# Turning two chunks of both heads with one full transpose in a hybrid encoder trunk

## The chip, the cores and the metric

The kernel runs on one core of a Trainium2 chip. A core has five engines that run their own instruction queues in order and meet at semaphores: TensorE (PE, matrix products into PSUM, with its weight loads shown apart as PEld), VectorE (DVE), ScalarE (ACT), GpSimd (POOL) and SyncE (SP, which here only issues DMAs). The metric is the time of one execution on the device, in microseconds. Three timed runs of the kernel before gave 1384.27 us as their median (1380.38 to 1386.24).

## The reference

Two layers act on 256 tokens of width 1024 in float32. Each is a half-step feed-forward block, a mixer, and another half-step feed-forward block. The mixer projects the normed input once and splits it in two branches:

```python
h = rms_norm(x, norm_mix[l]); proj = h @ w_in[l]
p_rwkv, p_attn, p_gate = jnp.split(proj, [C_RWKV, C_RWKV + C_ATTN], axis=-1)
o_a = rwkv7_mixer(p_rwkv, ...)      # 8 heads of 64, forward and backward scan
o_b = diff_attention(p_attn, ...)   # 4 heads, two softmaxes each
x = x + merged(sigmoid(p_gate), o_a, o_b) @ w_out[l]
```

The change lies in the RWKV-7 branch. Per head a 64 x 64 state runs over the tokens: `state = state * w + (state @ -kk) (kk * a)^T + v k^T` and `y = state @ r`, once in each direction.

## The kernel before, in words

**Layout.** Activations lie with features on the 128 partitions and the 256 tokens along the free axis. Large products are done as three fp32r products (high by high, low by high, high by low; `mm3`, lines 169 to 171). The weights come by DMA, ACT rounds the high part (`wh`, line 139) and DVE takes the low part (`wl`, line 144), or a DMA brings it (`low`, line 142).

**The RWKV branch.** Tokens are cut in 4 chunks of 64, heads are taken in 4 pairs `p` (two heads fill 128 partitions), and directions are `d` = 0 and 1. So a layer has 8 units (p, d). A unit has a front (`unit_front`: decays by `cum`, line 403, exponentials on ACT, lines 406 and 407, scaled tiles `bw`, `kw` and `ar` on DVE) and a back (`unit_back`). The back makes two PSUM tiles of products of `bw` and `kw` with `ar` (line 362, 64 x 64 stationary, the two heads in opposite corners of the array), which DVE masks into `ab`, `qb`, `ak` and `qk`; and it turns `bw` and `kw` so that tokens of a chunk lie on the partitions. `turn` (line 368) does it by a product with the identity, one for each tile, chunk and head: 16 a unit. One ACT copy (line 453) takes the result from PSUM to `wt`. `rwkv_v` does the same for `v`: 8 products for each of 4 pairs, and one copy (line 344) to `vt`.

**What follows.** When all units' `ab` are there, they go by DMA through DRAM into another layout (`gather_blocks`), DVE inverts triangular blocks (`invert`, lines 490 and 491), DMAs bring them back, `merge_blocks` does products on PE, and `chain` runs the four chunks, where `wt` (lines 578 and 580) and `vt` (line 561) are first read. Attention (`attention`: projections on lines 679 to 681, transposes on line 698, norms on lines 688 to 694; `attention_core`, lines 715 to 752) and gate tiles (`gates`, line 767 on DVE and line 768 on ACT) are independent work.

**What sets the order.** Parts are named in a plan (`PLANS`) with priorities (`PRS`), and a scheduler sorts all instructions into the engines' queues by a simulated timeline. So an edit of one part can move other parts. PSUM tiles come from small pools (`NB`): `acc` 3 buffers, `gen` 2, `att` 1, `back` 2.

In what follows a layer's mixer is spoken of in three stretches: the front stretch (first to last product of line 362 into a `back` tile), the inversion (until the first product of line 362 into a `gen` tile) and the chain (until the first branch product that reads `lora`).

Of the kernel before, what the change touches and what calls it, by code (L numbers as in the profile page):

```python
# [19 lines left out]
AF = mybir.ActivationFunctionType  # L20
# [4 lines left out]
P = 128  # L25
D = 1024
S = 256
# [31 lines left out]
class Trunk:  # L59
# [275 lines left out]
    def rwkv_v(self, l, q):  # L335

        nc = self.nc
        v = self.tmp("vv", [P, 2, S], bufs=1)
        self.shifted(l, [8 + 2 * q, 9 + 2 * q], [v[:, 0], v[:, 1]])
        for i in range(2):  # L340
            ps = self.gen()
            for c in range(4):
                self.turn(ps[:, c * 64:c * 64 + 64], v[:, i, c * 64:c * 64 + 64])
            nc.scalar.activation(self.vt[:, 2 * q + i], ps[:, :S].rearrange("p (c s) -> p c s", c=4), AF.Copy)

    def rwkv_pair(self, p):

# [16 lines left out]
    def turn(self, out, a):  # L364

        for h in range(2):
            r = slice(h * 64, h * 64 + 64)
            self.nc.tensor.matmul(out[r], a[r], self.ident[r, r], start=True, stop=True)  # L368

    def pair_front(self, p, k, r):  # L370
        nc, vec, mm = self.nc, self.vl, self.nc.tensor.matmul

        kk, sq = self.t1(), self.t1()
        nc.vector.tensor_scalar(kk, k, vec[:, V_KK + p:V_KK + p + 1], None, ALU.mult)
        nc.scalar.activation(sq, kk, AF.Square)
        ps = self.gen()
        for t in range(2):
            mm(ps[:, 2 * t:2 * t + 2], sq[:, t * P:(t + 1) * P], self.hind, start=True, stop=True)
        m = self.tmp("m", [P, 4])
        nc.vector.tensor_scalar(m, ps[:, 0:4], 1e-24, None, ALU.max)  # L380
        nc.vector.reciprocal(m, m)
        mb = self.t1().rearrange("p (a b c) -> p a b c", a=2, b=2)
        nc.vector.tensor_copy(mb, m.rearrange("p (a b) -> p a b", a=2).unsqueeze(3).to_broadcast([P, 2, 2, 64]))
        ps = self.gen()
        for t in range(2):
            mm(ps[:, t * P:(t + 1) * P], mb[:, t].rearrange("p a b -> p (a b)"), self.ident, start=True, stop=True)
        bm = self.t1()
        nc.vector.scalar_tensor_tensor(bm, ps[:, :S], -0.5, kk, ALU.mult, ALU.mult)
        return k, r, kk, bm, self.t1()
# [37 lines left out]
    def unit_back(self, p, d, st, bw, kw):  # L427
        nc = self.nc
        ar, ks = self.ar[d][:, p], st[4]
        c4 = lambda t: t.rearrange("p (c s) -> p c s", c=4)  # L430
        p1, p2 = self.back(), self.back()
        b4 = lambda t: t.rearrange("p (c a s) -> p c a s", c=4, a=2)
        for c in range(4):
            self.quads(p1[:, c * P:(c + 1) * P], bw[:, c * 64:c * 64 + 64], ar[:, c].rearrange("p a s -> p (a s)"))
        for c in range(4):
            self.quads(p2[:, c * P:(c + 1) * P], kw[:, c * 64:c * 64 + 64], ar[:, c].rearrange("p a s -> p (a s)"))
        mk = lambda i: self.masks[:, i:i + 1].to_broadcast([P, 4, 64])
        mi = (0, 1, 0, 1) if d == 0 else (0, 2, 3, 4)
        nc.vector.tensor_tensor(self.ab[:, p // 2, d, p % 2], b4(p1)[:, :, 0], mk(mi[0]), ALU.mult)
        nc.vector.tensor_tensor(self.qb[:, p // 2, d, p % 2], b4(p1)[:, :, 1], mk(mi[1]), ALU.mult)  # L440
        p3 = self.back()
        for c in range(4):
            cs = slice(c * 64, c * 64 + 64)
            self.turn(p3[:, cs], bw[:, cs])
            self.turn(p3[:, S + c * 64:S + c * 64 + 64], kw[:, cs])
        nc.vector.tensor_tensor(self.ak[:, p // 2, d, p % 2], b4(p2)[:, :, 0], mk(mi[2]), ALU.mult)
        if d == 0:
            nc.vector.tensor_tensor(self.qk[:, p], b4(p2)[:, :, 1], mk(mi[3]), ALU.mult)
        else:
            q = self.t1()  # L450
            nc.vector.tensor_tensor(c4(q), b4(p2)[:, :, 1], mk(mi[3]), ALU.mult)
            nc.vector.tensor_tensor(self.qk[:, p], self.qk[:, p], c4(q), ALU.add)
        nc.scalar.activation(self.wt[d][:, p], p3.rearrange("p (a c s) -> p a c s", a=2, c=4), AF.Copy)
        if d == 1:

            ps = self.gen()
            for c in range(4):
                for h in range(2):
                    q = slice(h * 64, h * 64 + 64)
                    nc.tensor.matmul(ps[q, c:c + 1], ks[q, c * 64:c * 64 + 64],  # L460
                                     self.vl[q, V_RK + p:V_RK + p + 1], start=True, stop=True)
            nc.vector.tensor_copy(self.bon[:, p], ps[:, 0:4])
# [491 lines left out]
```

## Time and profile before

| | us |
|---|---|
| median of three timed runs | 1384.27 |
| the profiled execution | 1376.89 |
| its span | 1375.1 |
| PE busy, of the span | 1335.4 |
| DVE busy | 908.3 |
| ACT busy | 702.9 |
| POOL busy | 226.9 |

The profile is of one execution. An engine's busy time is the time in which at least one instruction of it shows as running; matmuls are pipelined, so how long one lasts and how far apart two start are different numbers. A product of line 368 shows as two records, a transpose of line 698 as one. The line of an instruction is that of the helper that issued it. The chain of waits follows back from the last instruction what released each step.

### The profile page before, as it was taken

How to read it: one execution, taken by the hardware profiler on the slowest of the kernel's cores; microseconds unless marked ns; L12 is line 12 of the kernel's file. 1: busy time of each engine (PE TensorE's matmuls, PEld its weight loads, DVE VectorE, ACT ScalarE, POOL GpSimd, SP SyncE). 2: the span in 40 equal slices, each digit the busy share in tenths (PEclk: the TensorE clock that was granted, in tenths of full speed). 3: DMA queues.
4: the chain of work that ended last, by engine and by line, in shares of the span. 5: the costliest groups of instructions: out<-in, count | busy, mean ns of one | idle time of the engine just before them, and what ended most of it. 6: DMA issues, size and time to landing. Idle time of an engine off the chain costs nothing.

```text
span 1375.1 us, 31077 instructions
## 1 busy us (share of the span) xinstructions
PE 1335.4 (97%) x12916; PEld 1277.1 (93%) x12916; DVE 908.3 (66%) x1389; ACT 702.9 (51%) x1105; POOL 226.9 (16%) x216
## 2 busy tenths in 40 slices
PE   5999999999999999999999999999989999999999
PEld 5999999998788899999999999988968889999998
DVE  4777767756837776665567776686593487766653
ACT  4655555544545455444446565564346454544442
POOL 2222113101301122221021220120001020222200
PEclk9999999999999999999999999999999999999999
DMA  7898886558822555556668999843697145555564
GB/s 236 290 306 298 292 318 217 166 181 257 254 97 84 185 197 196 182 181 179 184 208 302 303 311 310 301 155 112 181 311 244 41 151 172 192 186 184 178 194 116
DMA packets 107549, 290.49 MB, mean 211 GB/s; under 512 B 31120, under 2 KB 37264, under 8 KB 106896
## 3 DMA queue, kind: packets, MB, share of 16 engines
q1 hardware_dynamic: 95856, 270.08, 60.2%
q10 hardware_dynamic: 11552, 18.42, 4.0%
q8 instruction: 101, 1.65, 0.5%
q14 instruction: 40, 0.33, 0.1%
HBM read 255.96 MB, written 32.51 MB: 210 GB/s over the span
## 4 chain that ended last, share of the span: by engine, by line
PE 88%; DVE 5%; DMA 2%; POOL 2%; ACT 1%; issue 1%; SPq 0%; ACTq 0%; DVEq 0%; POOLq 0%
PE acc L171 25%; PE acc L170 24%; PE acc L169 24%; PE back L362 2%; DVE tv L490 2%; PE att L715 1%; PE gen L362 1%; PE back L368 1%; DVE lora L491 1%; PE gen L399 1%; PE acc L681 1%; PE gen L403 1%; DMA wr<-f1i 1%; PE acc L679 1%; PE acc L680 1%
## 5 line engine op out<-in xcount | busy, mean ns | idle before, releaser
L169 PE MATMUL acc<-xh,wh 128*128 128x256 f32 x1904 | 542.8, 285 | 16.2 <-ACT wh L139 14.2
L139 ACT ACTIVATE wh<-wr 128x1024 fp32r<-128x1024 f32 (+1 forms) x390 | 402.8, 1036 | 287.8 <-PE acc L170 171.7
L171 PE MATMUL acc<-xh,wl 128*128 128x256 f32 x1904 | 543.9, 286 | 0.5 <-DVE wl L144 0.5
L170 PE MATMUL acc<-xl,wh 128*128 128x256 f32 x1904 | 542.2, 285 | 0.0
L144 DVE TENSOR_TENSOR wl<-wr,wh 128x1024 fp32r<-128x1024 f32 (+1 forms) x350 | 431.3, 1235 | 147.9 <-ACT wh L139 144.1
L169 PEld LDWEIGHTS acc<-xh,wh 128*128 128x128 f32 x1904 | 366.3, 192 | 20.0 <-ACT wh L139 14.2
L171 PEld LDWEIGHTS acc<-xh,wl 128*128 128x128 f32 x1904 | 366.0, 192 | 6.8 <-issue 4.9
L170 PEld LDWEIGHTS acc<-xl,wh 128*128 128x128 f32 x1904 | 366.3, 192 | 4.3 <-issue 3.9
L232 POOL TENSOR_TENSOR t<-t,t 128x256 f32<-128x256 f32 x88 | 112.3, 1277 | 386.6 <-ACT t L230 386.6
L171 PE MATMUL acc<-ar,wl 128*128 128x256 f32 x512 | 145.0, 283 | 0.0
L169 PE MATMUL acc<-ar,wh 128*128 128x256 f32 x512 | 144.9, 283 | 0.0
L170 PE MATMUL acc<-wt,wh 128*128 128x256 f32 x384 | 108.4, 283 | 0.0
L171 PEld LDWEIGHTS acc<-ar,wl 128*128 128x128 f32 x512 | 98.3, 192 | 0.1
L169 PEld LDWEIGHTS acc<-ar,wh 128*128 128x128 f32 x512 | 98.3, 192 | 0.0
L169 PE MATMUL acc<-wt,wh 128*128 128x256 f32 x320 | 89.8, 284 | 0.9 <-ACT wh L139 0.9
L171 PE MATMUL acc<-wt,wl 128*128 128x256 f32 x320 | 90.3, 284 | 0.2 <-DVE wl L144 0.2
L190 POOL TENSOR_TENSOR vv<-vv,t 128x256 f32<-128x256 f32 x42 | 39.1, 930 | 264.3 <-ACT t L189 263.7
L161 DVE TENSOR_TENSOR qk<-kr 128x1024 fp32r<-128x1024 f32 x40 | 49.0, 1225 | 47.2 <-ACT kr L159 47.2
L170 PEld LDWEIGHTS acc<-wt,wh 128*128 128x128 f32 x384 | 73.7, 192 | 0.1
L170 PE MATMUL acc<-ab,wh 128*128 128x256 f32 x256 | 72.4, 283 | 0.0
L159 ACT ACTIVATE kr<-kr 128x1024 fp32r<-128x1024 f32 x40 | 42.4, 1059 | 56.1 <-DMA kr<-win 28.3
L225 DVE TENSOR_TENSOR t<-acc,rs 128x512 f32<-128x512 f32 x88 | 60.2, 686 | 11.4 <-PE acc L171 10.9
(236 smaller groups left out, 1938.0 us busy)
## 6 DMA issues: line engine op xcount, KB each, us to landing
wr<-f1i SPq DMA_DIRECT2D x88, 512.0 KB, 5.2
wr<-f2i SPq DMA_DIRECT2D x88, 512.0 KB, 3.6
wr<-win SPq DMA_DIRECT2D x62, 512.0 KB, 4.4
low<-qk SPq DMA_DIRECT2D x40, 512.0 KB, 3.9
wl<-low SPq DMA_DIRECT2D x40, 512.0 KB, 5.0
wr<-f1o SPq DMA_DIRECT2D x32, 512.0 KB, 5.0
wr<-f2o SPq DMA_DIRECT2D x32, 512.0 KB, 3.7
kr<-watt SPq DMA_DIRECT2D x24, 512.0 KB, 5.7
```

Of the source, the lines that this page charges most:

```text
L139: nc.scalar.activation(wh[:, :n], raw[:, :n], AF.Copy)
L144: nc.vector.tensor_tensor(wl[:, :n], raw[:, :n], wh[:, :n].bitcast(F32), ALU.subtract)
L159: nc.scalar.activation(rw[:, 1].bitcast(F32R), rw[:, 0], AF.Copy)
L161: nc.vector.tensor_tensor(wl, rw[:, 0], rw[:, 1], ALU.subtract)
L169: mm(out, wh, xh, start=first, stop=False)
L170: mm(out, wh, xl, start=False, stop=False)
L171: mm(out, wl, xh, start=False, stop=last)
L190: nc.gpsimd.tensor_tensor(self.sq, self.sq, sq, ALU.add)
L225: nc.vector.tensor_tensor(gu, ps.rearrange("p (a b) -> p a b", a=2), self.rs.unsqueeze(1).to_broadcast([P, 2, S]), ALU.mult)
L232: nc.gpsimd.tensor_tensor(h, s, gu[:, 1], ALU.mult)
L362: self.nc.tensor.matmul(out[r], a[r], b[r], start=start, stop=stop)
L490: mul = lambda o, a, b: nc.vector.tensor_tensor(o, a, b, ALU.mult)
```

## The change

`turned` takes a list of tiles [128, 256] and, for every two chunks, turns the whole 128 x 128 block at once by a transpose. In the result the two chunks lie on the two halves of the partitions and the two heads side by side along the free axis, so that four ACT copies, each from one half of the partitions and one head to one half and one chunk, put the pieces where one copy put them before. Its call in `unit_back` stands behind the masks, while the products stood between them.

```diff
@@ rwkv_v
             ps = self.gen()
-            for c in range(4):
-                self.turn(ps[:, c * 64:c * 64 + 64], v[:, i, c * 64:c * 64 + 64])
-            nc.scalar.activation(self.vt[:, 2 * q + i], ps[:, :S].rearrange("p (c s) -> p c s", c=4), AF.Copy)
+            self.turned(self.vt[:, 2 * q + i:2 * q + i + 1], [v[:, i]], ps)
@@
+    def turned(self, dst, src, ps):
+        nc, n = self.nc, len(src)
+        for a in range(n):
+            for c in range(2):
+                at = a * S + c * P
+                nc.tensor.transpose(ps[:, at:at + P], src[a][:, c * P:c * P + P], self.ident)
+        f = ps[:, :n * S].rearrange("p (a c h s) -> p a c h s", a=n, c=2, h=2)
+        t = dst.rearrange("p a (c b) s -> p a c b s", b=2)
+        half = lambda i: slice(i * 64, i * 64 + 64)
+        for b in range(2):
+            for h in range(2):
+                nc.scalar.activation(t[half(h), :, :, b], f[half(b), :, :, h], AF.Copy)
@@ unit_back
-        p3 = self.back()
-        for c in range(4):
-            cs = slice(c * 64, c * 64 + 64)
-            self.turn(p3[:, cs], bw[:, cs])
-            self.turn(p3[:, S + c * 64:S + c * 64 + 64], kw[:, cs])
@@
-        nc.scalar.activation(self.wt[d][:, p], p3.rearrange("p (a c s) -> p a c s", a=2, c=4), AF.Copy)
+        self.turned(self.wt[d][:, p], [bw, kw], self.back())
```

The scheduler's order moves too. On PE, in the front stretch of layer 0, this stands at the first unit before (`t_457` is `bw`, `t_458` is `kw`, `back_3017` their PSUM tile):

```order
L169 MATMUL acc_3192<-xh_1861,wh_3225 128x256
L378 MATMUL gen_3041<-hind,t_474_3038 128x2
L368 MATMUL back_3017<-ident,t_457_2953 64x64 x2
L368 MATMUL back_3017<-ident,t_458_2954 64x64 x2
...
L378 MATMUL gen_3041<-hind,t_474_3038 128x2
L362 MATMUL back_3077<-ar_411_2714,t_464_2975 64x128 x8
```

and now:

```order
L169 MATMUL acc_3165<-xh_1861,wh_3198 128x256
L390 MATMUL gen_3032<-hind,t_474_3029 128x2
L374 MATMUL back_3019<-ident,t_457_2953 128x128 x2
L374 MATMUL back_3019<-ident,t_458_2954 128x128 x2
L390 MATMUL gen_3032<-hind,t_474_3029 128x2
L360 MATMUL back_3068<-ar_411_2714,t_464_2975 64x128 x8
```

The place in the row is the same; 16 products have become 4 transposes. On ACT, at the end of the same stretch, before:

```order
L453 ACTIVATE wt_412_2715<-back_3654 128x512
L139 ACTIVATE wh_4262<-wr_4260 128x1024
L453 ACTIVATE wt_413_2716<-back_3694 128x512
L139 ACTIVATE wh_4280<-wr_4278 128x1024
L267 ACTIVATE vv_4077<-t_645_4139,mu_105 128x256 x2
```

and now:

```order
L380 ACTIVATE wt_412_2715<-back_3596 64x4x64 x4
L380 ACTIVATE wt_413_2716<-back_3629 64x4x64 x4
L139 ACTIVATE wh_4214<-wr_4212 128x1024
L380 ACTIVATE vt_2721<-gen_4070 64x2x64 x4
L380 ACTIVATE vt_2721<-gen_4077 64x2x64 x4
```

Each copy has become four in a row; a weight tile (`wh`) that was rounded between the two copies to `wt` now stands behind both, and the copies to `vt` have moved up, closer behind them. On DVE, in the middle of the inversion of layer 1 (`tv` and `lora` are the inversion's tiles, `gg` a gate tile, `n` and `f` the norm of an attention tile), before:

```order
L490 TENSOR_TENSOR tv_12235<-lora_11816 128x1024
L491 TENSOR_REDUCE lora_11816<-tv_12235 128x4x16
L767 TENSOR_TENSOR gg_12538<-acc_12507,rs_10961 128x256
L490 TENSOR_TENSOR tv_12235<-lora_11816 128x768
L491 TENSOR_REDUCE lora_11816<-tv_12235 128x4x16
L490 TENSOR_TENSOR tv_12235<-lora_11816 128x512
```

and now:

```order
L497 TENSOR_TENSOR tv_12067<-lora_11690 128x1024
L701 TENSOR_TENSOR f_1963_12555<-f_1963_12555,n_1966_12560 128x512
L699 TENSOR_SCALAR n_1970_12575<-n_1970_12575 128x8
L498 TENSOR_REDUCE lora_11690<-tv_12067 128x4x16
L497 TENSOR_TENSOR tv_12067<-lora_11690 128x768
L701 TENSOR_TENSOR f_1968_12571<-f_1968_12571,n_1971_12576 128x512
```

Of five gate tiles that stood in this inversion one is left there, and the rest have moved ahead of it; the scalings of four attention tiles by their norms (line 701, line 694 before), which came behind it, stand inside it.

## Rows read from the trace of the kernel before

**Rows 1.** The page, busy time of engines
```profile
PE 1335.4 (97%) x12916; PEld 1277.1 (93%) x12916; DVE 908.3 (66%) x1389; ACT 702.9 (51%) x1105; POOL 226.9 (16%) x216
```
**Rows 2.** The stretches of both layers: each engine's busy time, clock, DMA
```profile
core 0: us, PE busy (x) PEld busy (x) DVE busy (x) ACT busy (x) POOL busy (x), PEclk, DMA share, GB/s
254.00:320.00 66.00, 66.00 (x852) 59.65 (x850) 40.94 (x123) 31.62 (x63) 5.18 (x7) 1.00 0.57 178
320.00:374.00 54.00, 50.20 (x336) 42.27 (x332) 42.17 (x73) 28.36 (x38) 11.42 (x5) 1.00 0.85 283
374.00:462.00 88.00, 84.24 (x1438) 74.41 (x1438) 52.06 (x116) 40.39 (x100) 8.43 (x10) 0.96 0.32 101
928.00:988.00 60.00, 58.29 (x815) 52.40 (x815) 40.40 (x119) 27.32 (x56) 6.27 (x8) 1.00 0.44 144
988.00:1047.00 59.00, 51.77 (x318) 42.91 (x314) 39.11 (x69) 29.17 (x37) 6.94 (x4) 0.97 0.88 281
1047.00:1146.00 99.00, 97.05 (x1565) 87.20 (x1564) 61.53 (x126) 46.73 (x108) 10.31 (x10) 1.00 0.41 130
```
**Rows 3.** Chain of waits in order of time: start, us, what
```profile
258.99 1.08 PE back L368 x32
...
977.10 0.93 PE back L368 x32
```
**Rows 4.** Waits of PE: what waited for what, total, times, longest
```profile
PE acc L169 <- ACT wh L139: 15.1, 3, 14.2
...
PE acc L679 <- DVE gg L767: 2.5, 2, 1.8
```
**Rows 5.** Groups of PE by shape: busy us, mean ns
```profile
L368 PE MATMUL back<-ident,t 64*64 64x64 f32 x512 | 20.8, 221 | 1.6 <-DVE qb L440 1.6
...
L698 PE MATMUL att<-ident,f 128*128 128x128 f32 x32 | 4.8, 274 | 3.2 <-DVE f L694 3.2
```
**Rows 6.** PE in order of time: start, us, what
```profile
276.72 0.28 PE L170 MATMUL acc<-xl,wh 128*128 128x256 f32 x1
276.84 0.28 PE L171 MATMUL acc<-xh,wl 128*128 128x256 f32 x1
...
277.89 0.61 PE L368 MATMUL gen<-ident,vv 64*64 64x64 f32 x14
278.34 0.22 PE L368 MATMUL back<-ident,t 64*64 64x64 f32 x1
```
**Rows 7.** PE in order of time, attention of layer 0
```profile
351.13 0.39 PE L681 MATMUL acc<-wl,xh 128*128 128x512 f32 x1
351.37 0.60 PE L698 MATMUL att<-ident,f 128*128 128x128 f32 x4
```
**Rows 8.** Chain of waits, a product with the identity
```profile
263.71 0.64 PE gen L386 x4
```
**Rows 9.** Groups of ACT by shape: busy us, mean ns
```profile
L453 ACT ACTIVATE wt<-back 128x512 f32<-128x512 f32 x16 | 9.5, 595 | 12.3 <-PE back L368 12.3
...
L740 ACT ACTIVATE tv<-att,n 128x128 f32<-128x128 f32 x16 | 5.8, 364 | 12.1 <-PE att L738 11.9
...
L344 ACT ACTIVATE vt<-gen 128x256 f32<-128x256 f32 x8 | 3.0, 381 | 9.8 <-PE gen L368 9.7
...
L540 ACT ACTIVATE sig<-back 32x512 f32<-32x512 f32 x4 | 2.3, 586 | 2.7 <-PE back L536 2.7
```
**Rows 10.** ACT in order of time, two instructions that read PSUM back to back
```profile
940.09 0.39 ACT L406 ACTIVATE e<-gen 128x260 f32<-128x260 f32 x1 [1.04 <-PE gen L403]
940.37 0.38 ACT L407 ACTIVATE e<-gen 128x260 f32<-128x260 f32 x1
```
**Rows 11.** ACT in order of time, last copy of layer 0 to `wt`
```profile
324.46 0.60 ACT L453 ACTIVATE wt<-back 128x512 f32<-128x512 f32 x1 [1.62 <-PE back L368]
```
**Rows 12.** Line 561, first reader of `vt`: ns min/median/max, first and last start
```profile
L561 PE MATMUL gen<-vt,ak x256: 218/218/268, 383.1 to 1125.1; 64*64 64x64 f32 x128
```
**Rows 13.** Group of POOL, the power in an attention norm
```profile
L693 POOL TENSOR_TENSOR n<-n,mhalf 128x8 f32<-128x8 f32 x8 | 17.3, 2162 | 75.9 <-DVE n L692 75.8
```

## Prediction

> **What bounds the kernel now.** I read the page's busy times first, then the same by stretch, then the waits of PE and the chain of waits. The reader is to see that PE is busy for 97% of the span, all other engines for at most 66% [rows 1], and that this holds in the mixer too, where all the changed work lies: in the front stretch of layer 0 PE is busy for 66.00 of 66 us, in that of layer 1 for 58.29 of 60 [rows 2]. ACT, which gets more work, is busy for 31.62 of 66 and 27.32 of 60 us there. Products of line 368 stand on the chain of waits themselves, 32 records at a time [rows 3], so what they take is, in the front stretches, paid in full. PE is not full everywhere: in the inversion it idles 54 - 50.20 = 3.8 us in layer 0 and 59 - 51.77 = 7.2 us in layer 1, in the chain 88 - 84.24 = 3.8 and 99 - 97.05 = 1.9 us [rows 2]. Waits of PE for a rounded weight tile come to 15.1 us in all, of which 14.2 are one wait, the first tile of the program, so 0.9 us are left for all the rest [rows 4].
>
> **What is removed on PE.** A unit's back had 16 products with the identity, each shown as two records. By the chain, 32 records go by in 1.08 us (layer 0) and 0.93 us (layer 1) [rows 3]; I take 1.0 us a unit. 16 units make 16.0 us. A call for `v` has 8 products, 16 records; 14 of them start within 278.34 - 277.89 = 0.45 us [rows 6], so 16 take 0.51 us, and 8 calls 4.1 us. Removed: 20.1 us.
>
> **What is added on PE.** 16 units x 4 + 8 calls x 2 = 80 transposes of 128 x 128. The same operation stands in the attention: four of them run from 351.37 for 0.60 us [rows 7], and one lasts 0.274 us [rows 5], so they start (0.60 - 0.27) / 3 = 0.11 us apart. 80 x 0.11 = 8.8 us. From both sides: four in 0.38 us would be the least (0.60 without the last one's tail of 0.22, as a record of line 368 has it [rows 6]), 7.6 us in all; the group's busy time, 4.8 us for 32, or 0.15 each, with nothing beside it [rows 5], gives 12.0 us. I keep 0.11, the row that is nearest in form. PE saves 20.1 - 8.8 = 11.3 us (8.1 to 12.5).
>
> **What is added on ACT.** Before: 16 copies of 0.595 and 8 of 0.381 us, 12.6 us [rows 9]. Now 64 copies of 64 x 256 and 32 of 64 x 128. That half of the partitions are used should save nothing: 32 x 512 takes 0.586 us where 128 x 512 takes 0.595 [rows 9]. So a 256-element copy is 0.381 us, and one of 128, by the step from 512 to 256 (0.214 for 256), 0.381 - 0.107 = 0.274; the slowest near row, 0.364, has a scale from memory as well [rows 9]. Together 24.4 + 8.8 = 33.2 us, 20.6 more (23.4 with 0.364). Back to back, reads of PSUM start 0.28 us apart while each lasts 0.38 [rows 10], which brings the addition down to 64 x 0.28 + 32 x 0.17 (0.28 less the 0.107 of 128 elements) - 12.6 = 10.8 us. [...]
>
> What hides it: each front stretch gets at most half of 23.4, 11.7 us, and ACT there is idle for 33 to 34 us [rows 2]. Nobody is in a hurry for the copies: the last one to `wt` of layer 0 begins at 324.46 [rows 11], and the first read of `vt`, with which the chain begins, is at 383.1 [rows 12]. What could be late is what stands behind the copies in ACT's queue, the rounding of weights and the exponentials of the next unit, and the PSUM tile itself, held for about 0.44 + 1.22 us (three steps of 0.28 and one copy of 0.38) where it was held for 1.0 + 0.6: the same. So I take zero; without that cover it costs the whole 20.6 us.
>
> **What the order moves.** Layer 0 keeps its shape: between the first and the last score product (line 362) stand 266 products of 256 columns where 247 stood, in the inversion 59 (66 before), in the chain 229 (241). Layer 1 moves more: 244 in the front stretch where 161 stood, 102 in the inversion (119, with 142 of 512 columns where 136 stood) and 208 in the chain (274 and 8 of 512 columns). At 0.12 us for 256 columns [rows 6] the front stretch gets 83 x 0.12 = 10.0 us of gate tiles, and the chain loses 66 x 0.12 + 8 x 0.24 [rows 7] = 9.8 us. PE's sum does not change by that, only its idle time. I read it from the layer whose order the new one resembles. The inversion of layer 1 idles 7.2 us, with waits for a gate tile's DVE step among them [rows 4]; now most gate tiles are ahead of it, as in layer 0, whose inversion idles 3.8 [rows 2]: -3.4 us. The chain of layer 1 idled 1.9 us with 274 products to fill it and that of layer 0 3.8 with 241, 0.06 us a product less; with 208 it idles some 5.8: +3.9. In layer 0, 12 products fewer: +0.7. Together +1.2 us, with an uncertainty of 4 either way, since the inversion also gets four scalings of attention tiles on DVE, which wait for a POOL step of 2.16 us [rows 13].
>
> **Sum.** -11.3 + 1.2 = -10.1 us. The profiled execution took 1376.89 us, so 1366.8 for one like it. The median of the timed runs is 7.4 us above that execution, and I put the difference on the median: 1384.3 - 10.1 = 1374.2, say 1374.
>
> **The rivals.**
> *The chain of layer 1 has a floor.* If its 99 us [rows 2] are set by its own succession of PE, ACT and DVE steps, the 9.8 us taken out of it turn to idle time, while its front stretch grows by 10.0 less the 5 saved there. Layer 0 gives 5.6, layer 1 loses 5: -0.6, and the time is 1383.7. For it: the chain's tiles go to and fro between engines. Against: layer 0's chain needs 88 us with 241 products [rows 2].
> *ACT becomes the limit (slower).* Place: the front stretches, where each unit's exponentials stand behind the four copies of the unit before. If all 20.6 us come onto PE's path, the sum is +9.3 and the time 1393.6; it decides from the point where over half of the copies' added time (11.3 of 20.6 us) is waited for. [...] For it: ACT's queue is in order. Against: 0.9 us of waits for rounded tiles, and ACT half idle.
> *The transpose is no cheaper than a float32 product.* Then it costs what line 386 does, 0.64 us for four records of two products [rows 8], 0.32 each: 80 x 0.32 = 25.6, +5.5 us, 1389.8. Against: line 698 shows one record for each and 0.11 us.
> *More than the turns.* If the inversion of layer 1 (59 us) comes down to layer 0's 54 and the chain's idle time does not grow, it is -11.3 - 5 = -16.3: 1368.
>
> **How the numbers follow.** Chances: forecast 0.50, floor 0.24, ACT 0.12, costly transpose 0.04, more than the turns 0.10. The forecast's own range is 1369 to 1381, by the bounds of the transposes (3 us) and of the idle time (4 us). The whole range is 1364 to 1389: it takes in the gain beyond the turns, the floor, and the lower half of the ACT case. A change of 0.5%, 6.9 us, is about what a measurement can tell from none. Faster than 1377.4: nine tenths of the forecast's chance, the whole of the last case and a little of the floor, 0.57; slower than 1391.2: the ACT case for the most part, and some of a mishap in the order, 0.13; the same: 0.30.
>
> **What would show it.** Right: line 374 with 80 records some 0.11 us apart; the front stretch of layer 0 ends about 2 us earlier, the chains of both layers are shorter, that of layer 1 by some 6 us or more; PE's busy time falls by about 11 us; line 380 with 96 copies of 0.27 to 0.38 us, and no wait of PE for `wh` beyond 2 us. Wrong: PE idle in the chain of layer 1 near 10 us (floor); PE or its weight loads waiting for ACT in the front stretches (ACT); 0.3 us between transposes; or an inversion of layer 1 longer than 59 us because its DVE steps wait for POOL.

## The result, and the profile after

The changed kernel takes 1393.2 us (median of 7, 1389.3 to 1404.7) against 1384.1 us of the kernel before: ratio 1.0102, with a 95% interval of 1.0072 to 1.0132. (The quotient of the two medians is only 1.0065; the ratio is taken from all runs, and those of the changed kernel spread upwards.) It is 1% slower, where 10 us less were forecast, and the time lies above the range.

In `after`, lines keep their numbers up to 341; `turn`'s product is line 366 (368 before), the score product 360 (362), lines 370 to 440 come 12 later, lines from 454 on 7 later. The page's busy times, to be held against [rows 1]:

```profile
PE 1331.4 (96%) x12356; PEld 1269.9 (92%) x12356; DVE 903.4 (65%) x1389; ACT 724.7 (52%) x1177; POOL 226.7 (16%) x216
```

ACT got 21.8 us more, as forecast (20.6). PE got 4.0 us less, not 11.3. The added work has the forecast price. Four transposes go by in 0.60 us, as the row of the forecast had it; below that row, for one line each: instructions, ns least, median and most, first and last start:

```profile
275.53 0.60 PE L374 MATMUL back<-ident,t 128*128 128x128 f32 x4
...
L374 PE MATMUL back<-ident,t x64: 270/273/421, 258.1 to 1005.6; 128*128 128x128 f32 x64
...
L380 ACT ACTIVATE wt<-back x64: 359/378/381, 258.8 to 1007.9; 64x256 f32<-64x256 f32 x64
L380 ACT ACTIVATE vt<-gen x32: 268/272/275, 278.8 to 1009.1; 64x128 f32<-64x128 f32 x32
```

So PE's missing gain is no dearer transpose. The six stretches, with the columns of [rows 2], and cut where the stages of this run end (the last turn of layer 0 is over at 479.6 us, before at 462.4):

```profile
254.00:320.00 66.00, 63.26 (x628) 56.80 (x626) 40.72 (x124) 42.51 (x92) 6.16 (x8) 1.00 0.65 211
320.00:374.00 54.00, 48.86 (x267) 40.03 (x267) 41.49 (x70) 27.48 (x41) 6.94 (x4) 0.94 0.72 245
374.00:480.00 106.00, 96.53 (x1513) 85.29 (x1512) 57.52 (x124) 43.57 (x103) 9.31 (x10) 0.94 0.35 108
939.00:1005.00 66.00, 63.34 (x658) 57.09 (x656) 41.76 (x123) 41.82 (x93) 6.18 (x8) 1.00 0.58 189
1005.00:1063.00 58.00, 53.18 (x280) 43.30 (x276) 44.00 (x73) 30.79 (x42) 9.89 (x4) 0.97 0.81 263
1063.00:1157.00 94.00, 85.56 (x1457) 76.38 (x1457) 52.27 (x116) 42.00 (x101) 9.49 (x10) 0.98 0.34 111
```

In [rows 2] layer 0's chain ends with its last turn, 6 us ahead of the first branch product that reads `lora` (468.5 us). In `after` the last turn stands behind that product (473.5 us), so the rows of 88 and of 106 us do not hold the same work. From the chain's first product to the last one that reads `lora` the work is nearly the same. This stretch before, and then after:

```profile
374.20:480.30 106.10, 102.34 (x1593) 92.65 (x1593) 67.17 (x136) 48.80 (x111) 8.43 (x10) 0.97 0.39 124
375.70:490.60 114.90, 104.63 (x1581) 93.48 (x1581) 63.60 (x132) 47.43 (x109) 9.31 (x10) 0.94 0.34 107
```

Two things are to be seen. The stretch is 8.8 us longer, and PE sits idle for 114.90 - 104.63 = 10.3 us in it, where it was 106.10 - 102.34 = 3.8. (Up to the first product that reads `lora`, the chain takes 97.8 us where it took 94.3.) And the granted clock is 0.94 in two stretches of layer 0 that had 1.00 and 0.96: PE spends more of its time at the lower level, 0.50, where an equal amount of work stands as more busy time (the records of the chain's last step, whose first four are shown below, go by four every 0.21 us at 0.50, in `after`, and four every 0.12 us at 1.00, before). One of those stretches, in the middle of the chain of layer 0:

```profile
448.40:455.20 6.80, 3.93 (x53) 3.45 (x53) 5.26 (x11) 1.10 (x2) 3.15 (x3) 0.51 0.41 118
```

The time from PE's first record to its last (1357.6 us before, 1369.9 after), less its idle time in between, less half of the time for which it was busy at 0.5, is an estimate of the work at full clock: 1329.2 us before, 1317.8 after. The work did fall, by 11.4 us. But idle time rose by 16.2 us, from 22.2 to 38.4, and what the half clock took rose by 7.5 us, from 6.2 to 13.7. The three terms, -11.4 + 16.2 + 7.5 = 12.3 us, are the difference of the two spans (1387.4 - 1375.1).

What PE waits for in the end of layer 0's mixer, after (in all, times, longest):

```profile
PE att L759 <- DVE tv L756: 4.4, 2, 4.1
PE acc L169 <- ACT lora L647: 1.6, 2, 1.2
PE acc L170 <- DVE lora L648: 1.1, 1, 1.1
```

The first is the attention core's last transposes. The two others are branch a, which needs the chain's end (`lora`). PE in order of time there, before (line 561 is the first product of a chain step, here of its last; line 752 the attention's last transposes):

```profile
441.54 0.28 PE L561 MATMUL gen<-vt,ak 64*64 64x64 f32 x4
...
446.87 0.60 PE L752 MATMUL att<-ident,tv 128*128 128x128 f32 x4
...
449.78 0.66 PE L752 MATMUL att<-ident,tv 128*128 128x128 f32 x4 [1.13 <-DVE icl L755]
```

and after (568 and 759):

```profile
446.15 0.63 PE L759 MATMUL att<-ident,tv 128*128 128x128 f32 x4 [0.28 <-DVE tv L756]
450.86 1.09 PE L759 MATMUL att<-ident,tv 128*128 128x128 f32 x4 [4.09 <-DVE tv L756]
452.35 1.12 PE L366 MATMUL gen<-ident,t 64*64 64x64 f32 x16 [0.40 <-DVE t L631]
453.26 0.42 PE L568 MATMUL gen<-vt,ak 64*64 64x64 f32 x4
```

The attention ends at about 450 us in both. But the chain's last step stood ahead of its transposes before, and stands behind them now: it starts 453.26 - 441.54 = 11.7 us later, after a wait of 4.1 us that it has nothing to do with, and its records last 0.42 us where they lasted 0.28, because the clock is at its lower level by then (0.50 from 452.3 to 455.1 us, where it was 1.00 from 441.5 to 444.7 us before).

### The profile page after: what moved, and what is told of

It reads as the page before. It is cut to its first block, busy times and chain, and to the rows that moved or that the text cites. A ratio compares the mean times of both kernels' runs of the same rounds, so it can differ in the third digit from the quotient of the medians.

```text
span 1387.4 us, 30032 instructions
## 1 busy us (share of the span) xinstructions
PE 1331.4 (96%) x12356; PEld 1269.9 (92%) x12356; DVE 903.4 (65%) x1389; ACT 724.7 (52%) x1177; POOL 226.7 (16%) x216
## 4 chain that ended last, share of the span: by engine, by line
PE 82%; DVE 8%; DMA 3%; issue 3%; ACT 2%; POOL 1%; SPq 1%; ACTq 0%; DVEq 0%; POOLq 0%
PE acc L170 24%; PE acc L171 24%; PE acc L169 24%; DVE tv L497 2%; PE back L360 2%; DVE lora L498 1%; DMA g<-gg 1%; PE att L722 1%; PE gen L411 1%; DVE wl L144 1%; DMA wr<-f1i 1%; ACT wh L139 1%; POOL vv L190 1%; DMA d<-ab 0%; PE gen L312 0%
## 5 line engine op out<-in xcount | busy, mean ns | idle before, releaser
L225 DVE TENSOR_TENSOR t<-acc,rs 128x512 f32<-128x512 f32 x88 | 60.2, 687 | 11.7 <-PE acc L171 11.5
```

The costliest lines, as they stand in the source:

```text
L225: nc.vector.tensor_tensor(gu, ps.rearrange("p (a b) -> p a b", a=2), self.rs.unsqueeze(1).to_broadcast([P, 2, S]), ALU.mult)
```

## The experiments

Three theories were set against each other. *Order*: the loss comes from the order that the scheduler makes of the new instructions. *ACT*: it comes from four copies in place of one. *Clock*: less PE work lets the granted clock fall. To part the instructions from their order, a kernel can have the order of each engine written out: behind the recording of the program, every instruction of an engine is tied behind the one that is to precede it. Shortened (the runs hold the orders packed):

```diff
+ORDER = {"PE": ..., "DVE": ..., "Activation": ..., "Pool": ..., "SP": ...}
+def freeze(tc, nc):
+    for e, at in ORDER.items():
+        own = [i for i in nc.cur_bb.bb.instructions if i.engine is e]
+        for a, b in zip(at, at[1:]):
+            tc.add_manual_dep(own[b], own[a].name, dep, reason="issue order")
...
         Trunk(ctx, tc, io).run(stages)
+        freeze(tc, nc)
```

Written-out orders change the number of instructions in the profiles by 6 at most (30032 in `after`, 30038 in the run of its instructions with most); no run has a kernel with its own order written out. Each ratio below is to the kernel before on the same chip, with its 95% interval. "Clock" is the mean of the granted clock over the timed runs (0.9964 for the kernel before, 109 runs). "Less the clock's share" is time less (1 - clock) x span, run by run, an estimate that takes all time at the lower level as half lost. In the first run below, whose times reach from 1375.8 us at 0.999 to 1389.0 us at 0.986, it leaves a spread of 6.8 of 13.2 us; in the 109 runs of the kernel before only 12.9 become 11.2 us.

**Instructions against order.**

Changed kernel, order of the kernel before (each engine's table is that of before, 4 transposes and 4 copies where the first of the products and the copy stood):

> The changed kernel's instructions, with every engine's order written out as it stands in the kernel before: the 4 (or 2) transposes stand where the first of the 16 (or 8) products stood, the 4 copies where the one copy stood, and nothing else moves. Order theory (the loss comes from the scheduler's new order, the edit itself saves PE time): 1384 - 10 = about 1374 us, 1370 to 1378. ACT theory (four copies instead of one delay the casts and exponentials queued behind them): 1384 or more, up to 1393. Clock theory (less PE work makes PE idle more often and the granted clock falls whatever the order): 1382 to 1393, with 20 us or more at granted clock 0.5 against 13.6 us in the kernel before.

1380.4 us, ratio 1.0002 (0.9982 to 1.0022), clock 0.9935. The order theory's direction holds, its number does not: the loss is gone, but so is the gain.

Kernel before, order of the changed kernel:

> The kernel before's instructions (16 or 8 products and one copy), with every engine's order written out as it stands in the changed kernel. Order theory: the new order's loss of some 19 us without the 10 us that the transposes save: about 1400 us, 1395 to 1406. ACT theory: the order is harmless and the copies are single again: 1384, 1381 to 1388. Clock theory: more PE work fills the gaps: 1384 to 1390.

1402.1 us, ratio 1.0145 (1.0121 to 1.0170), clock 0.9885. The old instructions lose 20 us by the new order alone. The ACT theory is out as the cause of the loss.

Kernel before in a third order:

> The kernel before's instructions (products, one copy) in a third order: the one that the scheduler makes when only the copies are cut in four. It stands about as far from the order before as the changed kernel's order does. If the order before is an especially good one and any other loses: 1390 to 1402 us. If the changed kernel's order is an especially bad one: 1380 to 1386.

1403.1 us, ratio 1.0164 (1.0141 to 1.0187). So the new order isn't exceptionally bad: another one loses as much. In this third order, too, the chain's last step has come behind the attention's last transposes:

```profile
455.97 0.68 PE L752 MATMUL att<-ident,tv 128*128 128x128 f32 x4
461.92 0.28 PE L561 MATMUL gen<-vt,ak 64*64 64x64 f32 x4
```

**The two parts of the edit, in the old order.** Transposes with one copy of all 128 partitions:

```diff
-        for b in range(2):
-            for h in range(2):
-                nc.scalar.activation(t[half(h), :, :, b], f[half(b), :, :, h], AF.Copy)
+        nc.scalar.activation(dst, ps[:, :n * S].rearrange("p (a c s) -> p a c s", a=n, c=4), AF.Copy)
```

> Order of the kernel before; transposes on PE, but one copy of 128 partitions instead of four (the halves are not put in place, so the values that follow are others; the amount of work after it is the same). Order theory: the PE part alone gives the whole saving, 1370 to 1377 us, within 2 us of the run with four copies in the same order. ACT theory: 1370 to 1377 as well, but at least 8 us below the run with four copies. Clock theory: 1382 to 1390.

1381.4 us, ratio 1.0001 (0.9985 to 1.0017), clock 0.9925. Less the clock's share it is 5.8 us faster than before; the lower clock takes 5.4 us back. And products with four copies (`f` and `t` are views of the PSUM tile and of `wt`, as in `turned`; the copy to `vt` is split in the same way):

```diff
-        nc.scalar.activation(self.wt[d][:, p], p3.rearrange("p (a c s) -> p a c s", a=2, c=4), AF.Copy)
+        for b in range(2):
+            for h in range(2):
+                nc.scalar.activation(t[half(h), :, :, b], f[half(h), :, :, b], AF.Copy)
```

> Order of the kernel before; the products with the identity as before, but their result copied in four pieces of 64 partitions (the ACT part alone, 20.6 us more ACT work by the prediction). Order theory: nothing waits for it, 1384 us, 1382 to 1387. ACT theory: 1393 us, 1390 to 1400. Clock theory: 1384, as PE's work is that of before.

1384.9 us, ratio 1.0024 (1.0007 to 1.0041), clock 0.9959: some 3 us (1 to 6 by the interval), a seventh of the added ACT time. In the profile 1.8 us of it show as waits of the next score products for a PSUM tile that the copies still read:

```profile
PE back L362 <- ACT wt L378: 1.8, 4, 0.6
```

**How much PE work the fronts give back.** In the old order, products doubled (`for _ in range(2)` about both calls of `turn`), one transpose for all, and transposes doubled:

> Order of the kernel before, one copy; each product with the identity is made twice, which adds 20.1 us of TensorE work in the two fronts (16 units of 1.0 us, 8 v calls of 0.51 us). If PE bounds the mixer: 1381.9 + 20 = 1402 us, 1399 to 1405. If the mixer's other engines or its transfers set half of its pace (the transposes gave 5.8 us of 11.3 us once the clock's share is taken off): 1392, 1388 to 1396. Clock theory (PE work in place of waits keeps the clock up): the mean granted clock is at or above that of the kernel before, 0.996.

> Order of the kernel before; a single transpose in place of the products, copied to all four places by one copy (most of what is turned is left out), so that TensorE has 17.5 us less to do than before and 6.2 us less than with the transposes. If PE bounds: 6 us under the run with transposes and one copy, about 1375 us at that run's clock. Floor theory (something else sets the pace once some 6 us are gone): 1380 to 1383, no gain over the transposes. Clock theory: a granted clock below 0.9925, and the time up to 1385.

> Order of the kernel before, one copy of 128 partitions (the halves are not put in place), every transpose made twice: 17.6 us of transposes stand where the kernel before has 20.1 us of products and the run with single transposes 8.8 us. If what counts for the clock is how much TensorE has to do: a mean granted clock of 0.995 to 0.997 as with the products, and 1378 to 1382 us. If transposes do not count as the products do: 0.990 to 0.993 as with single transposes, and 1384 to 1389 us. [...]

| PE work of the turning | ratio to before | clock | less the clock's share |
|---|---|---|---|
| products twice, +20.1 us | 1.0097 (1.0075 to 1.0119) | 0.9977 | +15.3 us |
| before | 1 | 0.9964 | 0 |
| transposes twice, -2.5 us | 0.9998 (0.9983 to 1.0014) | 0.9963 | -0.6 us |
| transposes, -11.3 us | 1.0001 (0.9985 to 1.0017) | 0.9925 | -5.8 us |
| one transpose, -17.5 us | 0.9982 (0.9964 to 1.0000) | 0.9917 | -8.7 us |

The first column goes by the prediction's costs. The one profile of each, split as above, has PE's work change by 18.2, -0.5, -8.7 and -15.1 us, and runs with the same instructions differ by a few us in this (1317.8 to 1323.4). So upwards three quarters of the work or more are paid, downwards a half to two thirds of it is given back, and the clock takes most of that (5.4 of 5.8 us, 6.5 of 8.7). The clock goes here with the amount of PE work, not with its kind: 17.6 us of transposes hold it (0.9963) where 20.1 us of products do (0.9964). At the third unit of layer 1's front PE waits 1.6 us ahead of its transposes in the profiles of single and of doubled transposes. Behind that wait the clock fell with single ones (first line) and held with doubled ones:

```profile
947.80:954.60 6.80, 6.78 (x56) 5.80 (x51) 2.15 (x7) 0.67 (x3) 0.00 (x0) 0.50 0.20 80
945.90:952.90 7.00, 6.58 (x79) 5.85 (x78) 2.81 (x10) 2.05 (x5) 0.00 (x0) 1.00 0.19 77
```

The doubling also took PE's idle time from 31.2 to 27.4 us over the run, and no run parts the two.

Where the rest stays can be read in the fronts and the inversions. Kernel before (a second profile, below) and the run with one transpose, front and inversion of layer 0, then of layer 1, columns as in [rows 2]:

```profile
254.70:323.70 69.00, 69.00 (x883) 62.63 (x884) 41.40 (x124) 33.02 (x63) 5.18 (x7) 1.00 0.59 185
324.00:374.90 50.90, 46.96 (x295) 38.71 (x290) 41.68 (x70) 27.04 (x36) 11.40 (x5) 1.00 0.84 278
929.00:989.40 60.40, 58.69 (x825) 52.92 (x826) 40.54 (x120) 27.56 (x56) 6.27 (x8) 1.00 0.44 143
989.70:1051.80 62.10, 53.06 (x310) 44.13 (x307) 40.80 (x69) 28.96 (x36) 6.93 (x4) 0.97 0.86 273
```

```profile
252.20:317.30 65.10, 63.10 (x637) 55.81 (x636) 41.08 (x124) 32.25 (x63) 5.19 (x7) 1.00 0.60 191
317.50:372.90 55.40, 49.04 (x236) 40.74 (x234) 41.84 (x70) 27.83 (x36) 11.38 (x5) 0.91 0.80 265
926.00:985.40 59.40, 55.28 (x553) 47.73 (x552) 40.90 (x120) 27.73 (x57) 6.28 (x8) 0.94 0.44 145
985.70:1046.80 61.10, 50.47 (x277) 41.75 (x277) 40.75 (x69) 28.60 (x35) 6.93 (x4) 1.00 0.85 279
```

PE's idle time in the inversions is 3.9 + 9.0 = 12.9 us before and 6.4 + 10.6 = 17.0 us with one transpose, at 82.5 and 82.6 us of DVE work: layer 0's front ends earlier, and PE then waits longer in the inversions, whose pace is set elsewhere. About as much is lost in the fronts themselves, where it is 0.0 + 1.7 = 1.7 us before and 2.0 + 4.1 = 6.1 us with one transpose: they are no longer full. With one transpose, over the whole run (before 4.4 us for the first, at its line 681):

```profile
PE acc L682 <- DMA wl<-low: 6.3, 4, 3.0
...
PE acc L169 <- DVE tv L491: 3.0, 1, 3.0
```

The kernel before once more:

> The kernel before, once more, for a second profile: its first profiled execution took 1376.9 us against a median of 1384. If that one was lucky in its waits, this one shows more than 22 us of PE idle time (28 to 32) at about the same granted clock; if not, 20 to 24 us.

1379.4 us, with 24.1 us of PE idle time against 22.2 in the first profile: that profile was not a lucky one to any extent that matters.

**Which layer.** The orders of both kernels have issued the same instructions when layer 0's second feed-forward part runs, so they can be cut and joined there.

```diff
-ORDER = {new order}
+ORDER = {old order up to layer 0's second feed-forward part, new order from there}    # and the mirror
```

> The changed kernel's instructions; layer 0's mixer in the order of the kernel before, layer 1's in the changed kernel's own order (cut inside layer 0's second feed-forward part, where both orders have issued the same instructions). If the new order loses in layer 0 alone, as the stages of the two profiles say (mixer of layer 0 10 us longer, of layer 1 2 us): 1381 to 1385 us. If both layers lose alike: 1387, 1385 to 1390. If layer 1 loses: 1390 or more.

> The mirror of the run above: layer 0's mixer in the changed kernel's own order, layer 1's in the order of the kernel before. If layer 0 alone loses: 1391 us, 1388 to 1396. If both lose alike: 1387. If layer 1 alone: 1381.

1381.8 us, ratio 1.0004 (0.9983 to 1.0026); the mirror 1392.5 us, ratio 1.0077 (1.0048 to 1.0107). As far as the runs can tell, the whole loss lies in layer 0 (1.0077 and the changed kernel's 1.0102 overlap). Layer 1, whose order moved most, loses nothing.

The clock is not a rival to the order here but a part of what the order costs. The changed kernel's mean clock is 0.9870 (7 runs), where its instructions in the old order have 0.9935. By means, the new order costs them 14.7 us (1396.3 against 1381.6); 9.2 of these are the clock's share by the estimate above, 5.5 are left when it is taken off. For the two joined orders it is 3.9 of 11.1 us.

**Which place in layer 0.**

```diff
+ORDER = {...}    # layer 0 as the scheduler orders the changed kernel with 'ac': -20 in PRS
+                 # (the kernel before with 'ac': 50), layer 1 in the old order
...
+        freeze(tc, nc)
```

`ac` is the attention core. `PRS` itself is as before in both runs; only the order that it makes is written out.

> The changed kernel's instructions. Layer 0's mixer stands in the order that the scheduler makes of them when the attention core's priority in that layer is lowered by 20: the front keeps the new order's 267 products of 256 columns (247 in the order before), but the chain's last step stands ahead of the attention core's last transposes again, as in the order before. Layer 1 is in the order before. To be read against the run with the new order in layer 0 and the old one in layer 1 (1392.5 us, 1.0077 of the kernel before). Theory (a), the chain's last step behind the attention's last transposes costs the time: 1380 to 1385 us, at most 1.003 of the kernel before. Theory (b), the products moved into the front are missing as cover later: 1389 to 1394 us.

> The kernel before's instructions and layer 1's order; layer 0's mixer in the order that the scheduler makes of them when the attention core's priority is raised by 50: the front keeps its 247 products, but the chain's last step now stands behind the attention core's last transposes, as in the changed kernel. Theory (a): 1391 to 1402 us, 1.007 to 1.015 of the kernel before. Theory (b): no loss, 1379 to 1384 us.

1383.7 us, ratio 1.0025 (1.0005 to 1.0046), and 1392.3 us, ratio 1.0082 (1.0054 to 1.0109). Both times are those of theory (a). PE in the first of the two:

```profile
451.03 0.28 PE L568 MATMUL gen<-vt,ak 64*64 64x64 f32 x4
...
454.05 0.66 PE L759 MATMUL att<-ident,tv 128*128 128x128 f32 x4
456.70 0.60 PE L759 MATMUL att<-ident,tv 128*128 128x128 f32 x4
```

and in the second, with a wait of branch a for the chain's end as in the changed kernel:

```profile
450.12 0.66 PE L752 MATMUL att<-ident,tv 128*128 128x128 f32 x4 [0.98 <-DVE icl L755]
458.27 0.42 PE L561 MATMUL gen<-vt,ak 64*64 64x64 f32 x4
```

```profile
PE acc L169 <- ACT lora L640: 3.0, 2, 1.8
```

The kernel before loses 12 us here with the products of its front in place, and the changed one is rid of 8 of its 11 us (1392.5 - 1381.1 = 11.4, 1383.7 - 1380.6 = 3.2, each against the kernel before on the same chip) with the new order's further products still in the front. Some 3 us are left for (b). All the traces go the same way: where the step stands behind the transposes (the changed kernel and four runs), the ratio is 1.0077 to 1.0164; where it stands ahead, it is 1.0025 at most, but for the products made twice. What is not shown is that the step alone does it. The scheduler moved more than that: of some 360 DVE instructions in layer 0's mixer, 46 stand elsewhere than in the new order in the first of the two, and 71 elsewhere than in the old order in the second, and no run moves the step by itself.

**Attempts at a faster kernel.** Two things were tried on the changed kernel in the old order. Moving real products ahead of three waits:

```diff
 # PE's order: six products ahead of the third group of L705 in layer 0,
 # four ahead of the third in layer 1, four ahead of the third group of L366
-L705 x4, L686..688 x6
+L686..688 x6, L705 x4
```

> The changed kernel's instructions in the order before, with three moves on PE: six products of the attention's projection ahead of the transposes that wait 1.85 us in layer 0's inversion, four ahead of those that wait 1.05 us in layer 1's, and four of branch b ahead of the turns that wait 1.16 us at the end of layer 0's chain. If these waits are idle time that other work can fill: 3 us less than the same kernel without the moves, 1377 us. If the waits only move on: 1380 to 1382. Clock theory adds: the granted clock goes up by 0.001 to 0.002.

1382.8 us, ratio 1.0006 (0.9984 to 1.0029), clock 0.9930. The wait of 1.85 us at the third group came down to 0.65, and nothing came of it: the waits moved on. And products that nothing reads, put into a wait of 2.4 us:

```diff
+    def dead(self):
+        ps = self.att()
+        for _ in range(8):
+            self.nc.tensor.matmul(ps[:, :S], self.xh[:, 0, :P], self.xh[:, 0], start=True, stop=True)
```

> The changed kernel's instructions in the order before, with eight products of 256 columns that nothing reads put into PE's stream in layer 1's front, where the third unit's transposes wait 2.4 us for a bank (a half-clock stretch of 13.7 us followed that wait in the profile). Clock theory (too little PE work in the front lets the clock fall): the mean granted clock rises above 0.9935 to 0.995 to 0.997, no half-clock stretch follows this wait, and the time falls by 2 to 5 us to 1376 to 1379. Otherwise: the clock as without them, and 1380 to 1383 us.

1380.9 us, ratio 0.9999 (0.9981 to 1.0018), clock 0.9941. In the two profiles the clock does what the theory says. Without them, before and after the wait:

```profile
936.00:950.00 14.00, 9.91 (x114) 7.88 (x113) 12.14 (x34) 9.33 (x22) 2.27 (x4) 1.00 0.32 113
950.20:963.90 13.70, 13.36 (x84) 11.74 (x85) 4.10 (x14) 5.61 (x17) 0.00 (x0) 0.50 0.10 39
```

and with them:

```profile
938.00:952.00 14.00, 10.83 (x119) 8.45 (x118) 12.15 (x36) 8.70 (x22) 2.27 (x4) 1.00 0.31 112
952.00:966.00 14.00, 12.63 (x119) 10.97 (x118) 4.15 (x14) 8.97 (x22) 0.00 (x0) 1.00 0.33 115
```

84 instructions go by in 13.7 us at the lower level, 119 in 14.0 at the higher (not all of the same shapes). But over twelve runs the mean clock is not measurably higher and the time is the same, so this is one place among several, and inconclusive for the whole. No version tried is faster than the kernel before by more than can be told.

## Why the prediction was wrong

*The step that failed* is "What the order moves". It put +1.2 us on the new order, +0.7 of it on layer 0, which "keeps its shape". The new order costs 20 us with the old instructions and about 11 us or more with the new ones, and as far as the runs can tell all of it lies in layer 0. In the two profiles PE's idle time rose by 16.2 us where 1.2 were forecast, and the half clock, for which there was no term, took 7.5 us more. The step counted products of 256 columns by stretch and read idle time from their number. What decided was, as far as shown, no number but a place: which of two chains' instructions stands first in PE's queue at the end of layer 0's mixer. The count in layer 0's chain moved by a twentieth, so it got 0.7 us, and layer 1, with 83 products more in its front, got terms of -3.4 and +3.9; the two layers cut and joined show that layer 0 is the one that matters.

*The sum's first term was right in work and wrong in time.* 11.3 us of PE work were to go: the records give 11.4 for the two first profiles, and transposes and copies have the durations that were worked out. It was taken as paid in full since PE is busy for 66.00 of 66 us in a front [rows 2]. In the old order, where nothing else moves, only 5.8 us come off at an equal clock, since fronts and inversions wait longer, and the clock takes 5.4 of them. That the fronts were full told here what it costs to add work there (15.3 of 20.1 us), less well what comes of taking it away (5.8 of 11.3 us). The clock stood in [rows 2] as a column, and no term of the sum used it.

*ACT's copies* were costed at nothing; they cost 3 us, at least in part by the PSUM tile that they hold longer (1.8 us of waits of score products), which the step had put at no change. The amount (20.6 us forecast, 21.8 measured) was right. At 3 us the copying was not the bottleneck.

*The rivals.* The ACT rival's time (1393.6 us) is the measured one to the microsecond, and its mechanism is wrong: four copies alone make 1384.9. The floor was looked for in layer 1's chain, and its sign came in good part: PE idles 94 - 85.56 = 8.4 us there in `after`, near the 10 that were named. But this layer loses nothing against the old order. The argument against this rival, a chain of 88 us in layer 0, rested on a row that ends with the last turn; up to the first product that reads `lora` the two chains took 94.3 and 94.0 us. Something like a floor does lie in the fronts and inversions, and in the old order the change is worth nothing (1.0002), near that rival's -0.6 us. The costly transpose is out. *The base* was fair in its profile, as the second one agrees with the first; its median of three was some 4 us above that of the 109 later runs (1380.6).

*Of the signs*, the 80 transposes, the copies and the waits for `wh` (2.0 us at most, but for the program's first tile) came as forecast. Layer 1's chain got shorter, but by 3 us and not 6 (94.0 to 91.0, up to the first product that reads `lora`). Layer 0's front did not end 2 us earlier (323.2 us in both), PE's busy time fell by 4.0 us and not 11, and layer 0's chain, which was to get shorter, got 3.5 us longer (8.8 with the products that read `lora`).

What stays open: whether the chain's last step alone makes the loss or other moves of the scheduler share in it; why the old order's chain of waits leaves just this much room in the inversions (transfers of `low` and DVE steps both show in the waits, and no run took one of them away), and which of several places lets the clock fall in a given run.

## What to carry to other kernels

Where a scheduler orders the work, a change of instruction counts is also a change of order: write out the old order for the new instructions, and the new order for the old ones, before either is given the credit. In a new order, look for in-order queues in which a step of one long chain has come to stand behind another chain's late instruction; here that went with more time (8 of 11 us in layer 0) than how many products lie in which stretch (some 3 us). And work taken out of a stretch that was full but had waits behind it bought here, in good part, idle time and a lower granted clock: of 11.3 us 5.8 came off at an equal clock, and the clock, at 0.9925 where it was 0.9964, took 5.4 of these.

## What was not expected of the hardware

In one and the same order the mean granted clock fell from 0.9977 to 0.9917 as PE work was taken out of two stretches of 60 to 70 us, and 8.8 us of transposes that nobody needed raised it from 0.9925 to 0.9963 and cost no time that can be told (1.0001 and 0.9998 of the kernel before). Runs of one kernel differ by up to 15 us, and the clock goes with a part of that: its share takes 6.4 of the 13.2 us in the changed instructions' runs in the old order, 1.7 of the 12.9 us in the kernel before's.
